# Regrouping the S5 branch of a hybrid layer by DMA through DRAM, with its convolutions, score chunks and decay selector rearranged

## Chip, cores and metric
The kernel runs on one core of one Trainium2 chip, as one program. The metric is the time of one execution on the device, in microseconds (us); the median of three executions is quoted.

## What is computed
A decoder layer for one sequence of 512 tokens with 1024 features: a gated feed-forward network, then a "hybrid mixer", then a second gated feed-forward network, each followed by a residual and a layer norm, and each modulated by a conditioning vector. The change lies in the mixer alone:

```python
proj = h @ w_in
z, xbc, dt_raw, u = split(proj)                    # 512 | 1024 | 8 | 512 columns
xbc = silu(causal_dwconv(xbc, conv_w, conv_b))     # 4 taps, per channel
xs, bm, cm = split(xbc)                            # 512 | 256 | 256
# SSD: chunks of 128 tokens, 8 heads; state passed from chunk to chunk
y_diag = (C B^T * exp(segsum(a*dt)))  @ (xs*dt)
y_off  = exp(cumsum(a*dt)) * C @ state_before
y_ssd  = rmsnorm((y_diag + y_off + d_ssd*xs) * silu(z)) * ssd_norm_w
# S5: 32 groups of 16 channels, 64 complex states each
x_t = A x_(t-1) + B u_t ;  y_t = Re(C x_t) + d*u_t
g = gelu(y_s5) ;  y_s5 = g * sigmoid(g @ w_glu + b_glu)
m = concat([y_ssd, y_s5]) @ w_out
```

All arrays are float32. Products of weights are made from a high and a low part (`split`, `mm3`): three matmuls in float32r for each product.

## The kernel before
The mixer (`mixer`, line 1248) holds features on the partitions and the 512 tokens along the row. A projection `proj()` makes one block of 128 columns of `w_in` for all tokens: 8 contraction tiles of 3 matmuls, into one PSUM bank. There are four such blocks for S5 (`u`), and eight for the convolutions (`conv(0)` to `conv(7)`; blocks 0 to 3 are `xs`, 4 and 5 `bm`, 6 and 7 `cm`).

S5 is worked four tokens at a time: 128 blocks of four tokens, so that one matmul contracts 4 tokens x 32 channels = 128 rows. For this the projected block, 128 channels x 512 tokens, must be regrouped to 4 tokens x 32 channels on the partitions, for each of four channel groups r. `s5_u` (line 930) does it with sixteen copies of 32 x 128 out of PSUM, twelve on ScalarE (L938) and four on VectorE (L940). `s5_scan` (line 942) makes eight matmuls (L949), a complex product with a rotation (`cmul`, three VectorE operations for each of the two parts), two scan instructions (L960) and a second `cmul`; its result X (two tiles, `bufs=1`) goes into `s5_y` (line 969): 48 matmuls (L978) that each load 32 columns of weights and write 32 PSUM partitions, so that the output lands in channel order, and one copy (L980). A float32 matmul is recorded as two passes. `s5_glu` (line 982) applies Gelu, splits, multiplies by `w_glu` (four contraction blocks into four banks) and applies Sigmoid.

For SSD, `ssd_dt` (line 1014) makes step sizes and decays; it is a generator that is advanced three times. `ssd_scores` (line 1117) makes for one chunk of 128 tokens C B^T, B transposed, and for each of two head groups a bank of decays: one matmul of the causal mask (L1132) and one with a selector of 64 rows (L1134: rows of `csel`, `acr`), then four Exp on ScalarE (L1137) and a product on VectorE. `ssd_x` transposes `xs`, `ssd_state` and `ssd_y` make state and output, `ssd_norm` and `ssd_out` the norm and the transposed result, which `out_proj` (line 1374) multiplies by `w_out`.

The text of `mixer` gives the order of priority: u, dt, u, scan, u, dt, scan, u, conv 4, dt, y0, conv 6, scan, conv 5, conv 7, y1, conv 0, scan, y2, conv 1, conv 2, y3 with Gelu, conv 3, then one chunk of scores, the gate product, and the other chunks. A planner fixes the order of each engine when the kernel is built: it takes, from what it holds to be ready by its own costs, what stands first in the text. `issue_after(i)` is an order on one engine only: what is traced in the block and runs on the engine of `i` is queued behind `i`. Each engine then works through its queue in order.

## Time and profile before

| | us |
|---|---|
| median of three executions | 966.65 (966.41 to 968.15) |
| profiled execution, its own time | 968.27 |
| its span, from the first to the last instruction | 966.6 |
| TensorE busy (98% of the span) | 944.9 |
| VectorE busy | 758.4 |
| ScalarE busy | 446.9 |
| GpSimd busy | 34.2 |

The mixer's part that the change touches runs from about 424 to 575 us of the span. Busy time of TensorE counts pipelined matmuls; how fast they follow each other is read from their start times in the timeline. In a timeline row the first number is the start, the second the duration from the first start to the last end of the instructions merged in the row, and brackets hold the idle time of the engine before it and what ended it. SPq and ACTq are the queues from which SyncE and ScalarE issue DMAs.

### The profile page before, as it was taken

The page shows a single profiled execution, that of the slowest core. Times are in us where ns is not written, and L with a number is a line of the kernel's source. Part 1 is how long each engine was busy: PE and PEld are TensorE (multiplying, and loading weights), DVE is VectorE, ACT ScalarE, POOL GpSimd, SP SyncE. Part 2 cuts the span into 40 slices and gives each one's busy share as a digit, 9 for nine tenths or more (in the row PEclk, how much of TensorE's full clock was granted, in tenths as well). Part 3 has the DMA queues.
Part 4 walks back from the last instruction along what each step waited for, and adds up shares of the span by engine and source line. Part 5 has one row for each costly group of instructions (what it writes and reads, how often), then busy time and mean ns, then how long its engine had stood idle before and what let it go on. Part 6 is the DMA issues. An engine that isn't in the chain of part 4 may idle for free.

```text
span 966.6 us, 14710 instructions
## 1 busy us (share of the span) xinstructions
PE 944.9 (98%) x5409; PEld 798.1 (83%) x5409; DVE 758.4 (78%) x1522; ACT 446.9 (46%) x879; POOL 34.2 (4%) x73
## 2 busy tenths in 40 slices
PE   8999999999999999999999999999999999999996
PEld 5778888887877888778877777988999999988885
DVE  6579998963677888858995889785788888896947
ACT  3343452635443335545537844533455554633420
POOL 0000000000000000100000110100000000000003
PEclk9999999999999999999999999999999999999999
DMA  9968584453866766362432024532233232543302
GB/s 342 377 190 270 188 280 162 157 174 122 261 204 197 242 217 180 86 233 71 142 121 67 1 88 152 173 111 66 88 99 120 89 129 90 175 152 109 109 1 87
DMA packets 75578, 147.93 MB, mean 153 GB/s; under 512 B 11633, under 2 KB 28657, under 8 KB 74993
## 3 DMA queue, kind: packets, MB, share of 16 engines
q1 hardware_dynamic: 75216, 146.94, 46.1%
q8 instruction: 42, 0.69, 0.3%
q14 instruction: 32, 0.25, 0.1%
q10 hardware_dynamic: 288, 0.04, 0.0%
HBM read 137.52 MB, written 9.44 MB: 152 GB/s over the span
## 4 chain that ended last, share of the span: by engine, by line
PE 86%; DVE 6%; ACT 4%; issue 2%; POOL 1%; DMA 0%; DVEq 0%; POOLq 0%; ACTq 0%
PE ps L103 27%; PE ps L104 27%; PE ps L105 27%; DVE cv L90 1%; PE ps L253 1%; PE ps L978 1%; DVE wlo L81 1%; PE ps L207 1%; ACT whi L96 1%; POOL rsx L170 1%; DVE s5X L81 0%; DMA raw<-in_w_in_dram 0%; PE ps L295 0%; DVE s5t L81 0%; PE ps L949 0%
## 5 line engine op out<-in xcount | busy, mean ns | idle before, releaser
L96 ACT CAST whi<-raw 128x1024 fp32r<-128x1024 f32 (+1 forms) x155 | 155.0, 1007 | 211.5 <-PE ps L104 97.5
L81 DVE TENSOR_TENSOR wlo<-raw,whi 128x1024 fp32r<-128x1024 f32 (+1 forms) x155 | 179.3, 1167 | 43.0 <-ACT whi L96 42.5
L103 PE MATMUL ps<-hT,whi 128*128 128x512 f32 x448 | 177.0, 396 | 1.7 <-ACT hT L1492 1.7
L104 PE MATMUL ps<-hT,whi 128*128 128x512 f32 x448 | 174.7, 390 | 0.1
L105 PE MATMUL ps<-hT,wlo 128*128 128x512 f32 x448 | 174.6, 390 | 0.0
L103 PE MATMUL ps<-whi,ghl 128*128 128x512 f32 x320 | 125.2, 391 | 0.0
L104 PE MATMUL ps<-wlo,ghl 128*128 128x512 f32 x320 | 124.5, 389 | 0.0
L105 PE MATMUL ps<-whi,ghl 128*128 128x512 f32 x320 | 124.3, 389 | 0.0
L103 PEld LDWEIGHTS ps<-hT,whi 128*128 128x128 f32 x448 | 83.9, 188 | 23.3 <-issue 3.2
L105 PEld LDWEIGHTS ps<-hT,wlo 128*128 128x128 f32 x448 | 84.1, 188 | 17.8
L104 PEld LDWEIGHTS ps<-hT,whi 128*128 128x128 f32 x448 | 84.2, 188 | 17.0 <-DVE hT L81 0.5
L103 PE MATMUL ps<-hx,whi 128*128 128x256 f32 (+1 forms) x320 | 97.5, 305 | 0.7 <-DVE cp L90 0.6
L104 PE MATMUL ps<-hx,whi 128*128 128x256 f32 (+1 forms) x320 | 97.3, 304 | 0.0
L105 PE MATMUL ps<-hx,wlo 128*128 128x256 f32 (+1 forms) x320 | 97.3, 304 | 0.0
L90 DVE SCALAR_TENSOR_TENSOR acc<-ra,cs,acc 128x1024 f32<-128x1024 f32 (+2 forms) x62 | 71.0, 1145 | 22.4 <-DMA ra<-in_w_ada_dram 21.9
L96 ACT CAST ghl<-g 128x512 fp32r<-128x512 f32 x88 | 53.1, 619 | 50.1 <-PE ps L105 37.5
L103 PEld LDWEIGHTS ps<-whi,ghl 128*128 128x128 f32 x320 | 60.1, 188 | 14.6 <-issue 2.5
L105 PEld LDWEIGHTS ps<-whi,ghl 128*128 128x128 f32 x320 | 60.1, 188 | 12.6
L104 PEld LDWEIGHTS ps<-wlo,ghl 128*128 128x128 f32 x320 | 60.1, 188 | 12.3
L81 DVE TENSOR_TENSOR ghl<-g,ghl 128x512 fp32r<-128x512 f32 x88 | 58.1, 686 | 13.6 <-ACT ghl L96 13.6
L103 PEld LDWEIGHTS ps<-hx,whi 128*128 128x128 f32 x320 | 61.1, 191 | 3.9 <-issue 0.8
L104 PEld LDWEIGHTS ps<-hx,whi 128*128 128x128 f32 x320 | 61.2, 191 | 2.6
(474 smaller groups left out, 1693.0 us busy)
## 6 DMA issues: line engine op xcount, KB each, us to landing
ra<-in_w_ada_dram SPq DMA_DIRECT2D x56, 512.0 KB, 4.5
raw<-in_up_dram SPq DMA_DIRECT2D x49, 512.0 KB, 4.2
raw<-in_ffn_w_dram SPq DMA_DIRECT2D x44, 512.0 KB, 4.4
raw<-in_up_dram SPq DMA_DIRECT2D x64, 256.0 KB, 3.8
ra<-in_ada_dram SPq DMA_DIRECT2D x16, 512.0 KB, 7.8
raw<-in_w_in_dram SPq DMA_DIRECT2D x16, 512.0 KB, 4.4
s5d<-s5mp SPq DMA_DIRECT2D x20, 256.0 KB, 3.8
s5M<-s5d SPq DMA_DIRECT2D x4, 1024.0 KB, 5.1
```

Source lines behind the costliest of these rows:

```text
L81: self.nc.vector.tensor_tensor(out=out, in0=a, in1=b, op=op)
L90: self.nc.vector.scalar_tensor_tensor(out=out, in0=a, scalar=s, in1=b, op0=op0, op1=op1, **k)
L96: keep(self.nc.scalar.copy(out=hi, in_=src))
L103: mm(o, lh, rh, start=first, stop=False, **k)
L104: mm(o, lh, rl, start=False, stop=False, **k)
L105: self.last_mm = mm(o, ll, rh, start=False, stop=last, **k)
L170: self.nc.gpsimd.tensor_scalar(out=x, in0=var, scalar1=EPS, scalar2=None, op0=ADD)
L207: self.nc.tensor.matmul(ps, self.onesr, bc(self.onesr, (1, 4)), start=True, stop=True)
L253: nc.tensor.matmul(bank[q:q + 32, 0:256], lhs, w[:, :, m * P:(m + 1) * P], start=(j < 2), stop=(j >= len(put) - 2))
L978: nc.tensor.matmul(pv[32 * r:32 * r + 32, j, :], M[:, n, r, 32 * j:32 * j + 32], rhs[:, r, :], start=(n == 0), stop=(n == 2))
```

## The change
- **Regrouping.** `s5_u` becomes one ScalarE copy of the bank (with tokens regrouped along the row) into a tile `s5c`, followed by `s5_turn`: one DMA of 256 KB from the ScalarE queue into a DRAM tile, and four DMAs of 64 KB from the GpSimd queue that read it back with 32 partitions each. `s5_y` becomes 12 matmuls with all 128 columns of weights, one copy, and the same turn; its result lands in the buffer of U, in regrouped order, and Gelu writes it into G in channel order.
- **Scan.** The constant tiles `d0` and X are made once; vr and vi take one buffer of the shared tag `t4` (two buffers) in place of tiles of their own.
- **Order.** Conv 4 and 6 stand between the second u and the first scan; the order is then scan, u, scan, u, conv 5, y0, scan, conv 7, conv 0, y1, scan, conv 1, y2, conv 2, conv 3, y3. Two chunks of scores stand ahead of the gate product, a third is queued behind the last Gelu; three Gelu are queued behind the Exp of the second chunk, and the Sigmoids behind the Exp of the last chunk. The weight loads are reordered to match.
- **Selector.** `acr` gets 128 rows for each head group, the other group's 64 rows filled with zeros (two more ScalarE operations), and L1134 uses all 128 rows.

```diff
+    def s5_turn(self, b, n, src, out):
+        d = self.s5_turns[b][:, n]
+        self.nc.scalar.dma_start(out=d, in_=src)
+        for j in range(4):
+            self.nc.gpsimd.dma_start(out=out[32 * j:32 * j + 32],
+                                     in_=d[:, j].rearrange("(r c) t -> c r t", r=4))
-    def s5_u(self, U, ups):
-        uv = ups.rearrange("p (t i) -> p i t", i=4)
-        for r in range(4):
-            for ii in range(4):
-                o, a = U[32 * ii:32 * ii + 32, r, :], uv[32 * r:32 * r + 32, ii, :]
-                if (r + ii) % 4 < 3:
-                    nc.scalar.copy(out=o, in_=a)
-                else:
-                    nc.vector.tensor_copy(o, a)
+    def s5_u(self, b, sp, U, ups):
+        c = sp.tile([P, 4, P], F32, tag="s5c", bufs=1, name=self.nm("s5c"))
+        self.nc.scalar.copy(out=c, in_=ups.rearrange("p (t i) -> p i t", i=4))
+        self.s5_turn(b, 0, c, U)
...
-        for j in range(4):
+        for r in range(4):
             for n, rhs in enumerate((U, X[0], X[1])):
-                for r in range(4):
-                    nc.tensor.matmul(pv[32 * r:32 * r + 32, j, :], M[:, n, r, 32 * j:32 * j + 32],
-                                     rhs[:, r, :], start=(n == 0), stop=(n == 2))
-        return nc.scalar.copy(out=G, in_=ps).ins
+                nc.tensor.matmul(ps[:, r, :], M[:, n, r, :], rhs[:, r, :], start=(n == 0), stop=(n == 2))
+        c = sp.tile([P, 4, P], F32, tag="s5c", bufs=1, name=self.nm("s5c"))
+        i = nc.scalar.copy(out=c, in_=ps).ins
+        self.s5_turn(b, 1, c, G)
...
+        def gelu(k):
+            return nc.scalar.activation(G[k].rearrange("p (t j) -> p j t", j=4), T[k], AF.Gelu_apprx_tanh).ins
         with self.tc.issue_after(after):
-            for k in range(4):
-                nc.scalar.activation(G[k], G[k], AF.Gelu_apprx_tanh)
+            gelu(0), gelu(1)
+            last = gelu(2)
         split(0), split(1)
+        with self.tc.issue_after(last):
+            self.last_gelu = gelu(3)
...
-            nc.scalar.activation(s, pss[o], AF.Sigmoid, bias=self.col["b_glu"][:, o:o + 1])
+            with self.tc.issue_after(self.last_exp):
+                nc.scalar.activation(s, pss[o], AF.Sigmoid, bias=self.col["b_glu"][:, o:o + 1])
...
-            gl = slice(64 * g, 64 * g + 64)
-            nc.tensor.matmul(ps, self.csel[gl, c, :], self.acr[gl], start=False, stop=True)
+            nc.tensor.matmul(ps, self.csel[:, c, :], self.acr[:, g], start=False, stop=True)
...
                 u()
+                next(dt)
+                conv(4)
+                conv(6)
                 scan()
                 u()
-                next(dt)
+                next(dt, None)
                 scan()
-                u(), conv(4)
-                next(dt, None)
+                u(), conv(5)
                 y(0)
-                conv(6)
                 scan()
-                conv(5), conv(7)
+                conv(7)
+                conv(0)
                 y(1)
-                conv(0)
                 scan()
+                conv(1)
                 y(2)
-                conv(1)
                 conv(2)
+                i = conv(3)
+                y(3)
                 mixT = []
-                glu = self.s5_glu(G, mixT, y(3))
-                next(glu)
-                i = conv(3)
...
                 with tc.issue_after(i):
                     scores()
+                scores()
+                glu = self.s5_glu(U, G, mixT, self.last_exp)
+                next(glu)
+                with tc.issue_after(self.last_gelu):
+                    scores()
+                tr()
                 next(glu), next(glu)
+                scores()
                 next(glu), next(glu)
-                tr()
-                scores(), scores()
```

## Rows read from the trace of the kernel before
**Rows 1.** The page's line of busy times by engine: busy us, share of the span, instructions.
```profile
PE 944.9 (98%) x5409; PEld 798.1 (83%) x5409; DVE 758.4 (78%) x1522; ACT 446.9 (46%) x879; POOL 34.2 (4%) x73
```
**Rows 2.** Busy time in chosen stretches: the stretch, its length, then busy us (and instructions) of PE, PEld, DVE, ACT, POOL, the granted TensorE clock as a share of full speed, the DMA share, GB/s.
```profile
424.20:513.10 88.90, 85.78 (x738) 70.49 (x736) 75.87 (x126) 43.68 (x93) 2.76 (x11) 0.98 0.41 142
513.10:546.60 33.50, 33.15 (x171) 25.21 (x168) 20.30 (x31) 30.37 (x65) 2.04 (x4) 1.00 0.10 32
...
480.00:492.80 12.80, 12.58 (x153) 10.42 (x153) 12.80 (x18) 6.49 (x9) 0.17 (x3) 1.00 0.24 72
495.30:499.20 3.90, 3.87 (x80) 3.72 (x80) 3.90 (x6) 1.30 (x2) 0.00 (x0) 0.58 0.55 188
```
**Rows 3.** What TensorE waited for between 425 and 600 us: us in total, times, longest.
```profile
PE ps L978 <- DVE s5X L81: 2.3, 2, 2.1
PE ps L1219 <- DVE zs L85: 1.9, 3, 0.7
```
**Rows 4.** TensorE's timeline at y1 (481.95), y2 (492.16) and y3 (510.35), with the projections that follow the first two and the scan before y2.
```profile
481.95 0.43 PE L978 MATMUL ps<-zx,s5M 128*32 128x128 f32 x8
...
484.71 0.50 PE L103 MATMUL ps<-hT,whi 128*128 128x512 f32 x1
...
490.28 1.95 PE L949 MATMUL ps<-zx,s5M 128*128 128x128 f32 x16
492.16 0.43 PE L978 MATMUL ps<-zx,s5M 128*32 128x128 f32 x8
...
495.33 0.65 PE L978 MATMUL ps<-s5X,s5M 128*32 128x128 f32 x8 [2.08 <-DVE s5X L81]
...
499.23 0.50 PE L103 MATMUL ps<-hT,whi 128*128 128x512 f32 x1
...
510.35 0.42 PE L978 MATMUL ps<-zx,s5M 128*32 128x128 f32 x8
```
**Rows 5.** TensorE's timeline at the first scan's matmuls, with the projection that follows.
```profile
440.26 1.95 PE L949 MATMUL ps<-zx,s5M 128*128 128x128 f32 x16
441.96 0.48 PE L103 MATMUL ps<-hT,whi 128*128 128x512 f32 x1
```
**Rows 6.** TensorE's timeline at the end of conv 3's projection and through the first chunk of scores.
```profile
518.45 0.39 PE L105 MATMUL ps<-hT,wlo 128*128 128x512 f32 x1
518.68 0.38 PE L1123 MATMUL ps<-zx 128*128 128x128 f32 x2
...
519.34 0.38 PE L1132 MATMUL ps<-mask,identb 128*128 128x512 bf16 x1
519.64 0.50 PE L1134 MATMUL ps<-acr,csel 64*128 64x512 f32 x1
520.08 0.39 PE L1132 MATMUL ps<-mask,identb 128*128 128x512 bf16 x1
```
**Rows 7.** TensorE's timeline from the state of one chunk (L1168) to the first product of the output projection.
```profile
542.87 1.03 PE L1168 MATMUL ps<-sx,bt 128*128 128x256 f32 x4
...
546.63 0.58 PE L103 MATMUL ps<-whi,mixT 128*128 128x512 f32 x1
```
**Rows 8.** ScalarE's timeline: three Gelu, conv 3's first pass, the first copy behind its Silu, the load of the Exp table and the Exp of the first chunk.
```profile
519.02 1.67 ACT L993 ACTIVATE zx<-zx 128x512 f32<-128x512 f32 x3
...
521.62 0.77 ACT L1111 ACTIVATE cv<-ps,cols 128x512 f32<-128x512 f32 x1
...
527.67 0.35 ACT L1127 COPY cbt<-ps 128x256 f32<-128x256 f32 x1
...
528.31 1.28 ACT L1137 ACT_TABLE_LOAD   x1
529.61 2.17 ACT L1137 ACTIVATE E<-ps,nacs 128x128 f32<-128x128 f32 x8
```
**Rows 9.** Groups of instructions by line between 424 and 513 us: line, engine, operation, tiles, shapes, count, then busy us, mean ns of one, idle time before them and what ended it; VectorE's first, then ScalarE's.
```profile
L940 DVE COPY zx<-ps 32x128 f32<-32x128 f32 x16 | 4.6, 287 | 1.6 <-ACT zx L938 1.2
L90 DVE SCALAR_TENSOR_TENSOR cv<-ps,cols,cv 128x510 f32<-128x510 f32 x6 | 4.5, 746 | 0.0
...
L938 ACT COPY zx<-ps 32x128 f32<-32x128 f32 x48 | 12.3, 256 | 11.4 <-DVE zx L940 10.9
```
**Rows 10.** Of the instructions that read the tile s5M, those of the scans' first product: min, median and max ns, first and last start.
```profile
L81 DVE TENSOR_TENSOR s5vr<-s5M,ps x4: 674/682/689, 442.9 to 496.9; 128x512 f32<-128x512 f32 x4
```
**Rows 11.** DMA issues of the whole execution: count, size, median us from issue to landing.
```profile
s5d<-s5mp SPq DMA_DIRECT2D x20, 256.0 KB, 3.8
...
s5d<-Er SPq DMA_DIRECT2D x4, 256.0 KB, 2.5
...
ew<-in_up_dram SPq DMA_DIRECT2D x2, 64.0 KB, 4.3
s_b_re<-in_s_b_re_dram SPq DMA_DIRECT2D x2, 64.0 KB, 2.9
```
**Rows 12.** GpSimd's timeline, the same operation on 128x2 elements twice, and what VectorE ran beside the first.
```profile
552.72 0.86 POOL L170 TENSOR_SCALAR rsx<-ss 128x2 f32<-128x2 f32 x1 [5.92 <-ACT jk L1207]
...
573.32 0.22 POOL L170 TENSOR_SCALAR rsx<-ss 128x2 f32<-128x2 f32 x1 [4.69 <-ACT jk L1207]
...
552.81 0.68 DVE L81 TENSOR_TENSOR y<-y,sx 128x512 f32<-128x512 f32 x1
574.36 0.62 DVE L85 TENSOR_SCALAR zs<-zs,ssr 128x256 f32<-128x256 f32 x2 [2.13 <-POOL ssr L171]
```

More of the change, by code (lines that the diff above doesn't have):

```diff
@@ L951, in s5_scan @@
         mk = lambda n: sp.tile([P, 4, P], F32, tag="s5" + n, bufs=1, name=self.nm("s5" + n))
-        d0, vr, vi = mk("d0"), mk("vr"), mk("vi")
+        if b == 0:
+            self.s5_d0, *self.s5_x = mk("d0"), mk("X0"), mk("X1")
+            for a in (self.s5_d0, *self.s5_x):
+                nc.gpsimd.memset(a[:, :, 0:1], 0.0)
+        d0, X = self.s5_d0, self.s5_x
+        v2 = self.tmp.tile([P, 1024], F32, tag="t4", name=self.nm("s5v")).rearrange("p (n r t) -> p n r t", n=2, r=4)
+        vr, vi = v2[:, 0], v2[:, 1]
         t = self.tmp.tile([P, 512], F32, tag="t2", name=self.nm("s5t")).rearrange("p (r t) -> p r t", r=4)
-        nc.scalar.copy(out=d0, in_=bc(self.s5_m4[:, 4 * b:4 * b + 4], (2, P)))
-        nc.gpsimd.memset(d0[:, :, 0:1], 0.0)
+        nc.scalar.copy(out=d0[:, :, 1:], in_=bc(self.s5_m4[:, 4 * b:4 * b + 4], (2, P - 1)))
         Er, Ei = M[:, 2], M[:, 3]
@@ L960, in s5_scan @@
             nc.vector.tensor_tensor_scan(out=fl(v), data0=fl(d0), data1=fl(v), initial=0.0, op0=MUL, op1=ADD)
-        X = [sp.tile([P, 4, P], F32, tag=f"s5X{n}", bufs=1, name=self.nm("s5X")) for n in range(2)]
-        for x in X:
-            nc.gpsimd.memset(x[:, :, 0:1], 0.0)
         s = slice(0, P - 1)
@@ L1082, in ssd_dt @@
         self.tt(bd, bc(pt, (1, NH)), bc(self.hsel, (2, P)), MUL)
-        self.acr = dp.tile([P, 4, P], F32R, name="acr")
+        self.acr = dp.tile([P, 2, 4, P], F32R, name="acr")
         for g in range(2):
-            self.split(bd[:, 4 * g:4 * g + 4], self.acr[64 * g:64 * g + 32], self.acr[64 * g + 32:64 * g + 64])
+            a = self.acr[:, g]
+            self.split(bd[:, 4 * g:4 * g + 4], a[64 * g:64 * g + 32], a[64 * g + 32:64 * g + 64])
+            o = slice(64 - 64 * g, 128 - 64 * g)
+            nc.scalar.mul(out=a[o], in_=bc(self.ones[o], (1, 4)), mul=0.0)
         self.dt, self.nacs, self.eacs, self.etot, self.dec = dt, nacs, eacs, etot, dec
@@ L1237, in want_mixer @@
                       self.zw_alloc)
-        cols = [1544 + b * P for b in range(4)] + [512 + b * P for b in (4, 6, 5, 7, 0, 1, 2, 3)]
+        cols = [1544, 1544 + P] + [512 + b * P for b in (4, 6)] + [1544 + b * P for b in (2, 3)]
+        cols += [512 + b * P for b in (5, 7, 0, 1, 2, 3)]
         for c0 in cols:
@@ L1294, in u @@
                     U.append(Ub[len(U)])
-                    self.s5_u(U[-1], proj())
+                    self.s5_u(len(U) - 1, sp, U[-1], proj())
                 def scan():
@@ L1302, in y @@
                 def y(b):
[L1303 removed]
+                    i = self.s5_y(b, sp, M[1][b], U[b], X[b], U[b])
                     load(1)
@@ L1355, in mixer @@
                 tr()
-                scores()
                 for _ in glu:
@@ L1527, in body @@
         L.s5_m4 = L.cp.tile([P, 16], F32, name="s5m4")
+        L.s5_turns = [tc.dram_tile([P, 2, 4, P], F32, name=f"s5t{b}") for b in range(4)]
         L.s5_dram = [tc.dram_tile([P, 7, 4, P], F32, name=f"s5d{b}") for b in range(4)]
```

13 lines of the change are left out of this document (6 added, 7 removed).

## Prediction
> **What bounds the kernel now.** The page comes first: TensorE is busy for 98% of the span [rows 1], so a change pays where it takes work from TensorE or closes one of the few places where TensorE waits; what leaves another engine pays only if TensorE waits for it. Next, the busy times by stretch over the mixer [rows 2]: from 424.2 to 513.1 TensorE is busy 85.78 of 88.90 us and VectorE 75.87, and from 480 VectorE has no idle time at all, so in this stretch both are close to the bound; from 513.1 to 546.6 TensorE is busy 33.15 of 33.50 us although ScalarE has 30.37 us of work there: the planner finds TensorE other work. Then the waits of TensorE [rows 3]: the largest is y2 waiting 2.3 us for the scan's result X on VectorE, then 1.9 us in three waits of the last transposes. Last, TensorE's timeline, where the starts of consecutive matmuls show what one really costs.
>
> **y2's wait.** y1 takes 484.71 - 481.95 = 2.76 us; y2 takes 499.23 - 492.16 = 7.07 [rows 4]. Of the 4.31 us between them 2.3 are the wait; the rest is the half-speed stretch behind it, with a granted clock of 0.58 of full speed from 495.3 to 499.2 [rows 2], between the levels of 1.2 and 2.4 GHz, after TensorE had stood for 2 us. In the new order two projections or more stand between a scan and its y, and VectorE loses the sixteen copies of L940, 4.6 us [rows 9]. Credit: **4.3**, if X is then in time.
>
> **Is it?** Before, VectorE's scan work began at 442.9 [rows 10], 2.6 us after the first scan's matmuls at 440.26 [rows 5], and y3 started at 510.35 [rows 4]. A projection takes 490.28 - 484.71 = 5.57 us [rows 4]. Conv 4 and 6 ahead of the first scan put it 2 x 5.57 = 11.1 us later; what VectorE need no longer do after that is 4.6 of copies and most of six convolution passes of 0.75, 4.5 [rows 9]. So the last X comes at 510.35 + 11.1 - 9.1 = 512.4. TensorE would be ready for y3 at 511.0 (next parts: conv 3 used to end at 518.68 [rows 6]; less 4.3 and 0.8 that gives 513.5 for y3's end, and 2.55 for y3). X is 1.4 us late, bounded by 0 and 5, since the count leaves out any idle time of VectorE. What is ready meanwhile is scores, which need only conv 4 to 7. I count nothing, and keep up to 3.6 as a rival.
>
> **y on full columns.** Before, 48 matmuls of 32 columns in 2.76 us [rows 4]. After, 12 matmuls, 24 passes; sixteen such passes take 441.96 - 440.26 = 1.70 us [rows 5], so 2.55. Four times 0.21: **0.8**. The lower end is 0, the column groups having run side by side already.
>
> **Selector.** From the mask matmul to the next pair is 520.08 - 519.34 = 0.74 us, of which 0.44 lie behind the 64-row matmul; a 512-column matmul on all rows passes in 518.68 - 518.45 = 0.23 [rows 6]. A pair on all rows should take 0.46. Eight pairs by 0.28: **2.2**. The lower end is 0 (the gap could come from the bfloat16 mask ahead). The Trainium skill, page "TensorEngine Tiling (Array Packing)", section "When to Use Tiling", speaks against this edit: at a contraction of 64 or less it advises two row tiles, up to twice as fast. Its "Key Properties" say that a change of tiling mode drains the engine, and the trace agrees with that: the two tiles never run side by side, a full-row mask matmul stands between them. By the first rule alone eight halves of 0.23 would be lost, 0.9, instead of 2.2 gained.
>
> **ScalarE and the small edits.** ScalarE loses 12.3 us of copies and 11.4 us of standing for VectorE between them [rows 9], and gets four copies of a whole bank and two of zeros. Gelu, Silu, Exp and Sigmoid no longer alternate: loads of 1.28 us [rows 8] fall away. TensorE waited for none of this but 0.35 us in 513.1 to 546.6 [rows 2], so the credit is 0; it shifts Exp and Sigmoid earlier. The tiles d0 and X made once free GpSimd of small memsets; vr and vi in `t4` share two buffers with the Gelu splits, which come after the scans. Weight loads on SyncE's queue follow the new order and stay ahead by the same count. All 0; uncovered, the zeros would cost about 1.2.
>
> **The turns.** None of this is in the trace: GpSimd issues no DMA before. A 256 KB write lands in 2.5 to 3.8 us, a 64 KB load in 2.9 to 4.3 [rows 11]. With a copy of 0.6, a turn takes from 6.0 (loads side by side) to 0.6 + 3.8 + 4 x 4.3 = 21.6 (one after another). I take 10, nearer to the first, as 64 KB loads need not wait for each other. Queued behind the wait: on ScalarE only what follows the write's issue, which waits for the copy just before it; on GpSimd, in order, the four loads behind the write's landing, with the later memsets of xd and the two selections for `csel` behind them; all of those are wanted tens of us later. SyncE's queue is passed by nothing. The cover for U is the order: between the third u's end and its scan TensorE has a scan, two projections and a y: 1.70 + 2 x 5.57 + 2.55 = 15.4 us; the other u have 18 or more. So 0, up to a turn of 15.4. Without that cover each turn would stand open, 10 us.
>
> **The new wait.** Conv 3 and y3 have changed places, and the gate product now waits for Exp. Call y3's end Z (513.5). Conv 3's projection ends at Z - 2.55. From there to its Silu's end took 527.67 - 518.68 = 9.0 us before [rows 6, 8], with a crowded ScalarE; free, it is a pass of 0.77, three of 0.75 and a Silu of about 0.6: 3.6. Behind it on ScalarE, in order: the Exp table 1.28, two chunks of 2.83 (copies from 527.67, Exp to 531.78, less the load), the Gelu table 1.28, three Gelu 1.67, a cast of 0.6 [rows 8]: 10.5. The first gate matmul comes at Z + 11.5 (to 17.0). TensorE's cover by the text's order is three score chunks, 0.66 + 2 x 0.46 = 1.6 each [rows 6], and four transposes: 5.2. That leaves a wait of 6.3 to 11.8. If the planner draws the fourth chunk and the state and output of two chunks forward, 3.76 each (542.87 to 546.63 [rows 7]), the cover is 13.8 and the wait 0 to 3.2. The full TensorE of 513.1 to 546.6 [rows 2] speaks for the second. I take **2.0**. Gelu 3, which waits for y3's turn, comes behind the other Gelu at Z + 11 and is needed only by the fourth quarter of the product.
>
> **Sum.** 4.3 + 0.8 + 2.2 - 2.0 = 5.3. The profiled execution took 968.27 with a span of 966.6, 1.6 above the median; I take the difference from the median: 966.65 - 5.3 = **961.4**.
>
> **Rivals.** (a) The gate wait takes the place of y2's: the planner keeps the text's order, or conv 3's Silu is late. Wait 6.3 to 11.8: 966 to 971, likeliest 967. Against: TensorE's filled stretch. (b) Slower: turns above 15.4 us, because GpSimd issues late beside VectorE. The same GpSimd operation took 0.22 us while VectorE stood and 0.86 while it added two tiles [rows 12]; VectorE is nearly full here. At 21.6 the third scan comes 6.2 late, Gelu 3 holds ScalarE and costs TensorE about 3, and the clock falls again, 2: 966.65 - 5.3 + 11.2 = 972.6. It decides from 15.4 on. The Trainium skill, "GPSIMD Engine Reference", section "Specifications", states this contention for VectorE instructions with two SBUF inputs, and "DMA: Bandwidth & Descriptors", "SWDGE vs HWDGE vs iDMA", that GpSimd writes descriptors into SBUF; that descriptors are slowed is shown by no row here. (c) VectorE becomes the bound: X late by 5 at y3, 3.6 of it uncovered: 965.0. (d) All waits close: no gate wait, and the 1.9 us of the last transposes [rows 3] go too, as Exp and Sigmoid end earlier: 966.65 - 7.3 - 1.9 = 957.4.
>
> **How the numbers follow.** Forecast (959 to 964) 0.50; (a) 0.16; (b) 0.12; (c) 0.10; (d) 0.12. The measurement tells about 0.2%, 1.9 us, from no change. Faster: 0.50, (d), half of (c) and a quarter of (a): 0.71. Same: half of (c), 0.07 of (a): 0.12. Slower: (b) and 0.05 of (a): 0.17. The range reaches from (d) into (a), 957 to 968; left out are (b) and the ends of (a) and (d), 0.19.
>
> **What would show it.** Right: TensorE's wait for X under 1 us and the clock at full speed through the scans; y in about 2.6 us; mask to next pair in about 0.46; turns of about 10 us; a gate wait near 2. Wrong: starts of scans that wait for a DMA, a gate wait above 6, or X later than y3's turn.

## The result, and the profile after

| | time, us | ratio to before, 95% interval |
|---|---|---|
| before, five runs | 966.95 (966.41 to 968.20) | |
| after, five runs | 978.64 (975.78 to 979.68) | 1.0111 (1.0090 to 1.0132) |
| forecast | 961.4 (957 to 968) | |

The change makes the kernel 11.7 us slower; the forecast had the sign wrong and the time lies outside its range. The profiled execution of after is the one of 975.78.

The page of after, its span and its busy line:

```profile
span 974.0 us, 14137 instructions
PE 939.9 (96%) x5121; PEld 797.0 (82%) x5121; DVE 752.7 (77%) x1506; ACT 434.8 (45%) x833; POOL 50.0 (5%) x96
```

Beside [rows 1] every large engine has less to do (TensorE too), and yet the span is longer: the time is in waits. Those of TensorE from 424 to 640 us (from the mixer to the transposes behind it), with total, count and longest:

```profile
PE ps L103 <- ACT ghl L96: 7.6, 1, 7.6
PE ps L979 <- DVE s5X L81: 3.3, 2, 3.1
PE ps L339 <- DVE res L87: 3.2, 2, 2.7
PE ps L104 <- DVE hx L81: 1.7, 1, 1.7
...
PE ps L1162 <- ACT E L1148: 0.9, 1, 0.9
...
PE ps L951 <- DMA zx<-s5t: 0.6, 1, 0.6
```

The waits of [rows 3] have not closed but moved: the gate product waits 7.6 us for a cast on ScalarE, a y waits 3.1 for X where y2 waited 2.3, and a third group (L339, L104) stands behind the mixer, of which the prediction says nothing. The turns, the new risk, cost one wait of 0.6. The busy times by stretch (columns as in [rows 2]):

```profile
440.00:450.00 10.00, 10.00 (x48) 8.34 (x47) 3.86 (x6) 3.51 (x6) 2.17 (x4) 1.00 0.55 157
470.00:516.00 46.00, 42.08 (x244) 36.23 (x245) 46.00 (x63) 15.75 (x22) 6.50 (x12) 1.00 0.54 168
521.00:530.30 9.30, 0.82 (x6) 0.43 (x5) 3.97 (x7) 9.27 (x24) 3.27 (x6) 0.69 0.18 47
530.30:534.70 4.40, 4.40 (x10) 3.19 (x11) 1.95 (x3) 4.37 (x10) 0.00 (x0) 0.50 0.00 0
```

VectorE has 3.86 us of work in the first ten and then no idle time at all for 46 us. TensorE stands in the third stretch while ScalarE is full, and in the fourth its granted clock is 0.50, the level of 1.2 GHz: the nine gate matmuls from 530.29 to 534.59 start 0.48 us apart in the mean, where 0.23 is usual [rows 6], which makes 2.2 us more. ScalarE's timeline shows what it does in that time:

```profile
518.34 0.63 ACT L1127 ACTIVATE zx<-cv 128x512 f32<-128x512 f32 x1 [1.06 <-DVE cv L90]
...
519.52 1.28 ACT L1148 ACT_TABLE_LOAD   x1
520.81 3.46 ACT L1148 ACTIVATE E<-ps,nacs 128x128 f32<-128x128 f32 x13
...
525.61 1.28 ACT L996 ACT_TABLE_LOAD   x1
526.90 2.90 ACT L996 ACTIVATE zx<-zx 128x512 f32<-128x512 f32 x3
529.61 1.14 ACT L96 CAST ghl<-zx 128x512 fp32r<-128x512 f32 x2
```

Conv 3's Silu (518.34) waits for VectorE; behind it in order come two chunks of Exp, the Gelu, and only then the cast that the gate needs. VectorE's timeline, the end of the second scan's X and conv 3's three passes, and TensorE's (a y that reads X, two pieces of the last y, two mask matmuls of one pair, the first gate matmul):

```profile
477.59 0.68 DVE L81 TENSOR_TENSOR s5X<-s5X,s5t 128x508 f32<-128x508 f32 x1
...
516.00 2.30 DVE L90 SCALAR_TENSOR_TENSOR cv<-ps,cols,cv 128x511 f32<-128x511 f32 x3
```

```profile
478.41 0.46 PE L979 MATMUL ps<-s5X,s5M 128*128 128x128 f32 x2 [3.08 <-DVE s5X L81]
...
514.93 0.39 PE L979 MATMUL ps<-zx,s5M 128*128 128x128 f32 x2
...
515.60 0.39 PE L979 MATMUL ps<-zx,s5M 128*128 128x128 f32 x2
...
516.94 0.38 PE L1144 MATMUL ps<-mask,identb 128*128 128x512 bf16 x1
...
517.39 0.39 PE L1144 MATMUL ps<-mask,identb 128*128 128x512 bf16 x1
...
530.29 0.79 PE L103 MATMUL ps<-ghl,whi 128*128 128x512 f32 x1 [7.62 <-ACT ghl L96]
```

The first of these y is that of scan 0, and it waits for scan 1's X. X is now one pair of tiles made in the first scan, and the text puts scan b+1 ahead of y b: so a y reads what the next scan has written (y3 excepted). This is a change of what is computed, not only of the order; it holds for the kernels made from after unless "own X" is said. The time does not hang on it: e2, which gives each scan its own X again, takes 978.33.

**Where the time went.** Each kernel enters the mixer at its own time (the first matmul of dt starts at 429.65 in before and 427.62 in after), so I count from that matmul (e8 shows where the difference comes from). Stages: to the first mask matmul (all projections, scans, y); from there to the output projection's first matmul (gate, chunks); from there to the end of the span. The first column is the start of the first scan's matmuls. The medians of before beside the experiments were 966.5 to 967.9.

| kernel | first scan at | scans | gate | rest | sum | median |
|---|---|---|---|---|---|---|
| before | 10.60 | 89.68 | 27.30 | 419.92 | 536.90 | 966.95 |
| after | 21.85 | 89.31 | 35.62 | 421.47 | 546.40 | 978.64 |
| e1 selector alone | 10.60 | 89.69 | 26.03 | 419.90 | 535.62 | 967.31 |
| e2 own X | 21.86 | 86.62 | 39.23 | 421.10 | 546.95 | 978.33 |
| e3 Gelu first | 21.86 | 89.35 | 34.48 | 422.00 | 545.83 | 977.25 |
| e4 no turns | 23.30 | 92.99 | 34.27 | 422.67 | 549.93 | 979.05 |
| e5 gate order back | 21.86 | 90.16 | 41.23 | 420.58 | 551.97 | 982.20 |
| e6 the same, own X | 21.86 | 89.38 | 36.49 | 421.68 | 547.55 | 978.31 |
| e7 splits held | 21.86 | 90.11 | 34.85 | 417.83 | 542.79 | 973.44 |
| e8 before again | 10.60 | 89.70 | 27.30 | 419.91 | 536.91 | 967.10 |
| e9 product first | 21.86 | 90.06 | 33.84 | 421.45 | 545.35 | 975.91 |
| e10 Gelu early | 21.86 | 90.10 | 33.23 | 422.18 | 545.51 | 975.81 |
| e11 early, own X, held | 21.86 | 86.62 | 34.68 | 418.71 | 540.01 | 971.06 |
| e12 order alone | 23.31 | 93.14 | 29.81 | 419.90 | 542.84 | 972.82 |
| e13 scan sooner | 16.42 | 88.22 | 36.18 | 421.01 | 545.42 | 976.41 |
| e14 sooner, own X, held | 16.41 | 84.92 | 32.74 | 419.24 | 536.90 | 968.10 |
| e15 Gelu at conv 1 | 16.41 | 84.93 | 32.73 | 418.68 | 536.34 | 967.79 |
| e16 before, u on ScalarE | 13.42 | 88.16 | 26.06 | 420.46 | 534.68 | 964.75 |
| e17 the same, not the first u | 10.63 | 85.41 | 26.08 | 420.47 | 531.96 | 961.83 |
| e18 the same, last two u | 10.62 | 86.67 | 26.20 | 420.48 | 533.35 | 963.53 |

After minus before is -0.37 + 8.32 + 1.55 = 9.50 us by stage. The other 2.2 of the 11.7 between the medians are in no stage shown here: after's profiled execution is its shortest, and it entered the mixer early, as e8's did.

Two kernels of the table lie between before and after, so the difference can be taken in three steps (scans, gate, rest, sum; us):

| step | scans | gate | rest | sum |
|---|---|---|---|---|
| before to e12: the new order of the scan stage | +3.46 | +2.51 | -0.02 | +5.94 |
| e12 to e4: the gate's new order, y3 behind conv 3, X made once, the selector | -0.15 | +4.46 | +2.77 | +7.09 |
| e4 to after: the turns and y on full columns in place of the copies | -3.68 | +1.35 | -1.20 | -3.53 |

The first two steps lose 13 us, and the turns give 3.5 of them back. The price of a step holds in this sequence; in another it could differ.

### The profile page after: what moved, and what is told of

Same layout as the page of the kernel before. It is cut to its first block, busy times and chain, and to the rows that moved or that the text cites. A ratio compares the mean times of both kernels' runs of the same rounds, so it can differ in the third digit from the quotient of the medians.

```text
span 974.0 us, 14137 instructions
## 1 busy us (share of the span) xinstructions
PE 939.9 (96%) x5121; PEld 797.0 (82%) x5121; DVE 752.7 (77%) x1506; ACT 434.8 (45%) x833; POOL 50.0 (5%) x96
## 4 chain that ended last, share of the span: by engine, by line
PE 78%; DVE 12%; issue 3%; DMA 3%; ACT 2%; POOL 1%; SPq 0%; DVEq 0%; POOLq 0%; ACTq 0%
PE ps L103 25%; PE ps L104 25%; PE ps L105 25%; DVE wlo L81 1%; DVE cv L90 1%; DVE s5v L967 1%; DVE s5v L81 1%; DVE s5t L81 1%; DMA ew<-in_up_dram 1%; DVE s5X L81 1%; DVE st L672 1%; DVE res L90 1%; DMA raw<-in_up_dram 1%; DVE res L87 1%; DMA b_ada<-in_badaT_dram 0%
## 5 line engine op out<-in xcount | busy, mean ns | idle before, releaser
L104 PE MATMUL ps<-hT,whi 128*128 128x512 f32 x448 | 174.9, 390 | 0.1
L104 PE MATMUL ps<-wlo,ghl 128*128 128x512 f32 x320 | 124.5, 389 | 0.0
L104 PEld LDWEIGHTS ps<-hT,whi 128*128 128x128 f32 x448 | 84.2, 188 | 17.0 <-DVE hT L81 0.5
L104 PE MATMUL ps<-hx,whi 128*128 128x256 f32 (+1 forms) x320 | 97.4, 304 | 0.0
L105 PEld LDWEIGHTS ps<-whi,ghl 128*128 128x128 f32 x320 | 60.0, 188 | 12.7
L104 PEld LDWEIGHTS ps<-wlo,ghl 128*128 128x128 f32 x320 | 60.1, 188 | 12.3
L103 PEld LDWEIGHTS ps<-hx,whi 128*128 128x128 f32 x320 | 61.1, 191 | 3.9 <-issue 0.8
L105 PEld LDWEIGHTS ps<-hx,wlo 128*128 128x128 f32 x320 | 61.1, 191 | 2.5
```

The costliest lines, as they stand in the source:

```text
L103: mm(o, lh, rh, start=first, stop=False, **k)
L104: mm(o, lh, rl, start=False, stop=False, **k)
L105: self.last_mm = mm(o, ll, rh, start=False, stop=last, **k)
```

## The experiments

**The theory after the result**: (i) ScalarE's queue, Exp ahead of Gelu, opens the gate's wait; (ii) a y tied to the next scan's X, and VectorE standing after 440 because the first scan comes later, take the gain of the scan stage; (iii) waits behind the mixer come from weight halves (of the next layer's weights). Rivals: the turns, or VectorE's or ScalarE's amount of work as such.

### e1, the selector alone, and e8, before once more

```diff
-            nc.tensor.matmul(ps, self.csel[gl, c, :], self.acr[gl], start=False, stop=True)
+            nc.tensor.matmul(ps, self.csel[:, c, :], self.acr[:, g], start=False, stop=True)
```

> The kernel before with the 128-row selector alone (its zeros included; the scans' vr and vi share the buffers of t4, as in the changed kernel, since the larger selector leaves no room for tiles of their own). Theory: the 0.44 us behind each 64-row matmul become 0.22, eight pairs give 2.2 us: 964.7. Rival 1: the gap came from the bfloat16 mask ahead, nothing changes: 967. Rival 2: half-row tiles were the better use of the array, 0.9 us slower: 968. The mask matmul to the next pair should show 0.46 in place of 0.74.

Measured: 967.31, ratio 0.9999 (0.9989 to 1.0009). In after a pair takes 517.39 - 516.94 = 0.45 us, as forecast, and TensorE's busy time in e1's profile is 2.27 less than in before's. But the stages give back only 1.28: TensorE's waits in the gate stage grow (for the gate's cast from 0.4 to 0.8 us, and 0.4 at a chunk's output). The medians do not show the 1.28; the two profiled executions, which enter the mixer within 0.06 us of each other, do: 967.04 against 968.27.

e8 is the kernel before, unchanged.

> The kernel before, profiled once more. Its waits around y2 and at the last transposes should stand as they did, and the span at 965 to 967; if stages move by more than 1 us between two profiles of the same kernel, differences of that size in the other profiles mean nothing.

Its stages agree with the first profile's to 0.02 us, its entry into the mixer does not: 427.89 against 429.65. The 1.7 us arise ahead of the mixer's change, at the projection of z, where TensorE waits 1.14 us in both; behind that wait the granted clock fell in the first profile (0.66 of full speed over the next 5 us, between its two levels of 1.2 and 2.4 GHz) and not in this one (1.00). Before's line, then e8's:

```profile
399.50:404.50 5.00, 5.00 (x15) 3.95 (x16) 4.36 (x8) 3.10 (x7) 1.02 (x2) 0.66 0.36 109
399.00:404.00 5.00, 4.78 (x21) 3.97 (x22) 4.68 (x9) 3.43 (x8) 0.70 (x2) 1.00 0.34 108
```

In all twenty profiles the ten matmuls behind that wait take either 2.2 us, and the mixer is entered at 427.6 to 428.4, or 3.3 to 3.8, and it is entered at 429.3 to 429.8, whatever the kernel: times can differ by about 1.7 us for this alone. Most of the 2.2 us above may be that; the executions without a profile do not show it.

The scan stage can move in the same way. e7, e9 and e10 leave after's scan stage as it is, and take 90.06 to 90.11 against 89.31: behind the first y's wait of about 3 us the granted clock fell in these three (0.67 or 0.68 over the next 5 us), and not in after and e3 (1.00). After's line, then e7's:

```profile
478.40:483.60 5.20, 5.19 (x34) 4.74 (x35) 5.20 (x9) 1.58 (x2) 0.00 (x0) 1.00 0.78 267
478.50:483.80 5.30, 5.25 (x21) 4.42 (x22) 5.30 (x9) 0.78 (x1) 0.00 (x0) 0.68 0.77 269
```

So in kernels with that wait, differences of up to 0.8 us in the scan stage mean nothing; elsewhere stages can be compared between single profiles more closely.

### e2, each scan its own X

```diff
...
-        d0, X = self.s5_d0, self.s5_x
+        d0 = self.s5_d0
...
+        X = [sp.tile([P, 4, P], F32, tag=f"s5X{n}", bufs=1, name=self.nm("s5X")) for n in range(2)]
+        for x in X:
+            nc.gpsimd.memset(x[:, :, 0:1], 0.0)
```

> The changed kernel, but each scan allocates its own X (one buffer, column 0 zeroed each time), as before the change. Theory: the waits of the first y come from its reading tiles that the next scan in the text writes; with tiles of its own y follows its own scan, and the 3.1 us wait goes: 975.5 (974 to 976.5), the gate's wait of 7.6 us unchanged. Rival: VectorE is simply late; the next scan's X waits for y to free the one buffer, the same microseconds come back as waits of the later y: 978 to 980.

Measured: 978.33, in the rival's range. The first y no longer waits and the scan stage is 2.69 us shorter, as the theory had it, though y2 now waits 2.0 for X; the gate stage is 3.61 longer, which neither said. ScalarE's line for conv 3's Silu:

```profile
519.09 0.63 ACT L1129 ACTIVATE zx<-cv 128x512 f32<-128x512 f32 x1 [1.53 <-DVE cv L90]
```

It starts 519.09 - 428.37 = 90.72 us after dt's first matmul, in after 518.34 - 427.62 = 90.72: to the hundredth the same, although TensorE ended its projections sooner: the Silu waits for VectorE, which makes conv 3's passes. The first gate matmul follows 11.95 us behind that Silu in both (531.04 and 530.29). What TensorE gains before is waited for at the gate.

### e3, Gelu ahead of Exp, and e9, the product ahead of the chunks too

```diff
...
-                with tc.issue_after(i):
+                glu = self.s5_glu(U, G, mixT, i)
+                next(glu)
+                with tc.issue_after(self.gelu2):
                     scores()
                 scores()
-                glu = self.s5_glu(U, G, mixT, self.last_exp)
                 next(glu)
```

> The changed kernel, but the first three Gelu go ahead of the Exp of the two chunks on ScalarE; the fourth Gelu goes behind those Exp. Theory: the gate product waits 7.6 us because ScalarE does 16 Exp and a table load ahead of the Gelu; with the Gelu first, the first gate matmul comes 7 to 8 us after the end of y3 in place of 14, with 5 to 6 us of other work of TensorE in between: the wait is 2 to 3, the stretch at half clock behind it goes, 970 to 972. Rival: ScalarE as a whole is the bound of this stretch, the Exp are then late for the states and outputs, and the wait only moves: 977 to 979.

Measured: 977.25, in the rival's range; of the gate's 35.62 us only 1.14 go. TensorE's timeline of e3:

```profile
522.28 0.58 PE L1146 MATMUL ps<-acr,csel 128*128 128x512 f32 x1
527.84 0.59 PE L1145 MATMUL ps<-mask,identb 128*128 128x512 bf16 x1 [4.98 <-ACT bt L1141]
...
530.30 1.12 PE L1163 MATMUL ps<-ident,zx 128*128 128x128 f32 x4 [1.44 <-ACT E L1149]
531.33 0.79 PE L103 MATMUL ps<-ghl,whi 128*128 128x512 f32 x1
```

The casts are there 5.6 us sooner (526.11 - 429.76 = 96.35 after dt, in after 529.61 - 427.62 = 101.99), but three chunks and the transposes lie ahead of the product in TensorE's own queue, and their banks come free only by ScalarE's copies, now behind the Gelu. e9 puts them behind the product as well:

```diff
...
-                with tc.issue_after(i):
-                    scores()
-                scores()
-                glu = self.s5_glu(U, G, mixT, self.last_exp)
-                next(glu)
+                self.conv3 = None
+                glu = self.s5_glu(U, G, mixT, i)
+                next(glu), next(glu)
                 with tc.issue_after(self.last_gelu):
                     scores()
+                next(glu), next(glu)
+                next(glu), next(glu)
                 tr()
-                next(glu), next(glu)
-                scores()
-                next(glu), next(glu)
+                scores(), scores()
...
```

> The changed kernel, its scan stage untouched; behind conv 3's Silu come all four Gelu, then the Exp, and TensorE has the gate product behind one chunk of scores, the other two chunks behind the product. Theory: e3 freed the Gelu alone and TensorE's queue held the product back; e5 held conv 3's Silu back instead. With both in order the first gate matmul comes about 8 us after the end of y3 (Silu 2.7, load 1.3, two Gelu 2.2, cast 0.6) with 1.6 to 2 of cover, a wait of 5 to 6 at once, but the Exp and the later chunks are then covered by the product: the state comes 3 us earlier, 974 to 976. Rival 1: Gelu 3 waits for the turn of y3 (11 us) and holds every Exp back in ScalarE's queue; the time is found again before the state: 978 to 981. Rival 2: the wait for the gate is lost whole (as I forecast at first): 970 to 972.

Measured: 975.91, inside the theory's range. The gate's waits are 5.0 in place of 7.6 and the first state matmul comes 3.8 sooner (113.74 after dt against 117.56), but the stage shortens by 1.78 only.

### e4, the new order without the turns

```diff
...
-        c = sp.tile([P, 4, P], F32, tag="s5c", bufs=1, name=self.nm("s5c"))
-        self.nc.scalar.copy(out=c, in_=ups.rearrange("p (t i) -> p i t", i=4))
-        self.s5_turn(b, 0, c, U)
...
+        for r in range(4):
+            for ii in range(4):
...
```

> The changed kernel in its order, but u and y regroup as before the change (sixteen copies of 32 partitions into U, y on column groups, Gelu in place), with no DMA through DRAM. Theory: the turns are hidden but for a wait of 0.6 us, and the copies cost VectorE 4.6 us again, so this is not faster: 978 to 981, waits for X longer than 3.1. Rival: the turns are the loss, by late U, by the transfers or by the Gelu with regrouped output: 968 to 973.

Measured: 979.05, in the theory's range, though the wait for X is 2.4 and not longer than 3.1. The scan stage is 3.68 us longer than in after and all three stages together 3.53: the turns cost less than the copies and column groups that they replace. They are not the loss.

### e5 and e6, the gate's order of before

```diff
...
-                i = conv(3)
-                y(3)
                 mixT = []
+                glu = self.s5_glu(U, G, mixT, y(3))
+                next(glu)
+                self.conv3 = conv(3)
+                next(glu)
...
```

> The changed kernel, but the gate goes back to its place of before: y3 ahead of conv 3, Gelu 0 and 1 ahead of conv 3's Silu, Gelu 2 and 3 right behind that Silu and ahead of the first Exp, one chunk of scores ahead of the gate product on TensorE and the other three after or within it. Theory: e3 gained little since TensorE's own queue still had three chunks of scores and four transposes ahead of the gate product, and their banks come free only by ScalarE; with the product first, it covers the Exp: no wait above 2 us at the gate, no half clock, 968 to 971 (the later waits of 3 stay). Rival: the stretch is bound by ScalarE's sum, or the turns of y2 and y3 (11 us) come too late for Gelu 2 and 3: the wait is found again inside the gate product, 975 to 978.

Measured: 982.20, slower than both. ScalarE's timeline of e5:

```profile
519.17 0.59 ACT L981 COPY s5c<-ps 128x512 f32<-128x512 f32 x1 [4.57 <-DMA s5t<-s5c]
...
531.59 1.28 ACT L1128 ACT_TABLE_LOAD   x1 [2.51 <-DVE cv L90]
...
534.83 2.04 ACT L996 ACTIVATE zx<-zx 128x512 f32<-128x512 f32 x2
```

y3's copy waits 4.57 us for the landing of y2's write, as both use the one buffer s5c; two Gelu, a Silu and three table loads behind it hold conv 3's first pass back to 527.37 and its Silu to 532.88, and Gelu 2 and 3, behind that Silu, hold the second half of the product. My theory was wrong here: the old order does not carry the turns. The gate's first wait is 6.5 us, and the product's second half comes late as well, as the rival said, but dearer than it said.

e6 is e5 with the edit of e2.

> As e5, and each scan has its own X (one buffer) as in e2. Theory: in e2 the scan stage ended 2.7 us earlier, and the gate gave it back because ScalarE's chain there, counted from conv 3, set the time; with the gate covered the 2.7 us stay: 2 to 3 us under e5, 965.5 to 968. Rival: the earlier end of the scans only lengthens the wait for the turns of y2 and y3 or for VectorE: same as e5 within 1 us.

Measured: 978.31: outside both ranges. Own X is worth 4.4 here in the sum, where y3's copy no longer waits for the landing of y2's write.

### e7, three weight halves behind the drain

```diff
...
-            ws = [(self.wnext(), self.wnext()) for _ in range(halves)]
+            with self.tc.issue_after(self.dr1[0]):
+                ws = [(self.wnext(), self.wnext()) for _ in range(halves)]
...
```

A drain is VectorE's work that takes a finished bank of the output projection into the residual; `dr1[0]` belongs to the first drain of the second half.

> The changed kernel, but three halves of the next layer's weights are kept behind the first drain of the second half of the output projection on VectorE (an order alone; nothing is left out). Theory: the waits of 2.7, 0.5 and 1.7 us at the transposes of res and at hx come from these halves, whose loads land late, in front of that drain: they shrink to about 1, and the kernel is 3 us faster: 975 to 976.5. Rival: the drains are late anyway, since the output projection itself ends late, or the weights are then late: 978 to 980.

In after VectorE's timeline ahead of the first drain of the second half reads:

```profile
592.72 1.22 DVE L81 TENSOR_TENSOR wg<-raw,wg 128x1024 fp32r<-128x1024 f32 x1 [0.72 <-ACT wg L96]
596.07 1.23 DVE L81 TENSOR_TENSOR wlo<-raw,whi 128x1024 fp32r<-128x1024 f32 x1 [2.12 <-ACT whi L96]
597.22 0.68 DVE L81 TENSOR_TENSOR dr<-ps,gate 128x512 f32<-128x512 f32 x1
```

Measured: 973.44, faster than the theory's range. The rest is 3.64 us shorter than in after, and the waits are

```profile
PE ps L339 <- DVE res L87: 0.5, 1, 0.5
PE ps L104 <- DVE hx L81: 0.4, 1, 0.4
```

in place of 3.2 and 1.7. The planner had drawn halves whose loads land late ahead of the drain (ScalarE waits 4.64 and 2.30 us for these loads). The change does not touch these lines; that their place moved because what stands ahead of them did is inferred, not tested.

### e10 and e11, Gelu early, and all three causes at once

```diff
...
-                conv(2)
-                i = conv(3)
+                mixT = []
+                glu = self.s5_glu(U, G, mixT, conv(2))
+                next(glu)
+                self.conv3 = conv(3)
                 y(3)
-                mixT = []
...
```

> As e9, but Gelu 0 and 1 go behind conv 2's Silu, ahead of conv 3's, since their turns have long landed; Gelu 2 and 3 behind conv 3's Silu, one chunk of scores ahead of the product. Theory: half of the product is ready when TensorE has ended y3, and covers the Silu, the other Gelu and the turn of y3: no wait above 1.5 us at its start, 1 to 3 within it: 969 to 972. Rival: two more table loads delay conv 3's Silu, and Gelu 3's wait for the turn of y3 holds the Exp: 975 to 978.

Measured: 975.81, the rival's range. The gate's wait is down to 1.6, but the later mask matmuls wait for Exp, and the gate stage is 33.23.

e11 is e10 with the edits of e2 and e7.

> e10 with the two other causes taken away as well: each scan its own X (e2) and the three halves of weights behind the first drain (e7). Theory, with the causes adding up: under e10 by 2.7 (own X, stays now that the gate is covered) and by 3.6 to 5 (splits): 962 to 966, level with the kernel before or faster. Rival: the gains overlap (an earlier end of the scans only waits longer for the turns): 967 to 970.

Measured: 971.06, ratio 1.0032 (1.0021 to 1.0043): above both ranges. Beside e10, own X takes 3.48 from the scans (0.8 of it is e10's fallen clock) and adds 1.45 to the gate; the held splits take 3.47 from the rest. Both causes are real, but taking them away does not make the kernel faster than before.

### e12, the order alone

```diff
...
                 u()
+                next(dt)
+                conv(4)
+                conv(6)
                 scan()
                 u()
-                next(dt)
+                next(dt, None)
                 scan()
...
```

> The kernel before with the new order of the scan stage alone: conv 4 and 6 ahead of the first scan, the other convolutions between a scan and its y; u and y regroup by copies and column groups, y3 ahead of conv 3, the gate and the selector as before. Theory: the projections between scan and y close the wait of y2 (2.3 us and 2 of half clock), but VectorE does the same work in the same stretch, and its first scan starts 11 us later: X comes late at the end instead, and the end of the scan stage moves by less than 1 us: 966 to 968. Rival: the order alone brings the 4.3 us that I credited to it: 962.5.

Measured: 972.82, ratio 1.0046 (1.0029 to 1.0063): outside both, slower. Lines of its waits and its busy times:

```profile
PE ps L978 <- DVE s5X L81: 4.1, 3, 2.2
...
PE ps L1060 <- DVE adt L90: 1.1, 1, 1.1
```

```profile
440.00:450.00 10.00, 8.94 (x42) 7.15 (x41) 5.06 (x15) 6.58 (x19) 0.00 (x0) 1.00 0.19 52
```

Before's line of the same stretch:

```profile
440.00:450.00 10.00, 10.00 (x64) 8.94 (x63) 9.55 (x21) 6.31 (x20) 0.00 (x0) 1.00 0.20 52
```

The order that was to close y2's wait makes three of it. VectorE has 5.06 us of work where before had 9.55, and is full from 490 to 516. The gate stage, whose order is that of before, is 2.51 us longer.

### e13 to e15, the first scan sooner

```diff
                 conv(4)
-                conv(6)
                 scan()
                 u()
                 next(dt, None)
+                conv(6)
                 scan()
```

> The changed kernel, but conv 6 goes behind the second u's scan instead of ahead of the first (its weights too), so that the first scan comes one projection, 5.6 us, sooner; U of the first scan still has 11 us for its turn. Theory: VectorE stood 6.1 us of the 10 from 440 to 450 and was full from 470 to 516; the sooner scan fills that hole, X and the convolutions of the end come 3 to 5 us sooner, conv 3's Silu and the gate with them: 973.5 to 976. Rival: what limits is the turns or the wait for the next scan's X, the hole is closed and nothing moves: 978 to 980.

```profile
440.00:450.00 10.00, 10.00 (x54) 8.56 (x53) 5.38 (x9) 2.38 (x7) 2.17 (x4) 1.00 0.54 157
```

```profile
517.42 0.63 ACT L1127 ACTIVATE zx<-cv 128x512 f32<-128x512 f32 x1 [1.07 <-DVE cv L90]
```

Measured: 976.41, the direction of the theory but less. VectorE does 1.52 us more in those ten, conv 3's Silu starts 517.42 - 428.00 = 89.42 after dt, 1.30 sooner, and the first gate matmul 1.29 sooner: what closes of the hole, a quarter of its 6.1 us, comes back almost whole.

e14 is e11 with this edit; e15 is e14 with Gelu 0 and 1 made behind conv(1) in place of conv(2).

> e11 with conv 6 behind the first scan. Theory as for e13: VectorE's late start was what e11 still paid: 3 to 5 us under e11's 971.1: 966 to 968. Rival: e11's rest (3 us over the kernel before) is the gate's 5.3 us wait for Gelu behind conv 2's Silu, and a sooner scan changes it by less than 1: 970 to 971.

Measured: 968.10, ratio 1.0001 (0.9992 to 1.0010): 3.0 under e11, a tenth above the theory's range. Its scans take 84.92, 4.76 less than before; the gate stage takes 5.44 more, with these waits among others:

```profile
PE ps L103 <- ACT ghl L96: 2.7, 1, 2.7
...
PE ps L1142 <- DVE y L81: 1.5, 1, 1.5
```

> e14, and Gelu 0 and 1 go behind conv 1's Silu in place of conv 2's, their casts later as the buffers come free. Theory: the gate's wait at its start goes, 2 to 4 us under e14: 963 to 966. Rival: the Gelu holds up the convolutions' Silu by two table loads of 1.28, no better than e14.

Measured: 967.79. The gate matmul starts 2.88 sooner and the gate stage is the same to 0.01: the rival. Wherever its first wait stood, the gate stage stayed at some 33 us in e10, e14 and e15; what holds it there was not tested.

### e16 to e18, VectorE relieved in the order of before

```diff
-                if (r + ii) % 4 < 3:
+                if late or (r + ii) % 4 < 3:
                     nc.scalar.copy(out=o, in_=a)
```

These are e17's and e18's lines: `late` is true for all but the first u in e17, for the last two in e18. In e16 the branch is gone, and ScalarE makes every copy. All three have e1's selector, so they are compared with e1.

> The kernel before with the 128-row selector (e1) and all sixteen copies of a u on ScalarE, four fewer on VectorE. No DMA, no new order. Theory: VectorE is relieved of 4.6 us in the stretch where it is full from 480 on, X of the third scan comes sooner, and y2's wait of 2.3 with the half clock behind it closes; U comes 1.2 us later where nothing waits for it: 2 to 4 us under e1: 962 to 965. Rival: the copies are longer on ScalarE alone, the scans themselves wait for U: 967 to 971.

Measured: 964.75, ratio 0.9966 (0.9954 to 0.9978), in the theory's range. y2's wait is gone; a wait at dt is new, behind the first u's copies on ScalarE:

```profile
430.61 4.27 ACT L937 COPY zx<-ps 32x128 f32<-32x128 f32 x16
434.90 0.57 ACT L1025 COPY dtfm<-ps 16x512 f32<-16x512 f32 x1
```

```profile
PE ps L1028 <- ACT dtfm L1025: 2.0, 1, 2.0
```

> e16, but the first u is copied by both engines as before the change, the other three by ScalarE alone. Theory: the 2.0 us wait of dt's matmul and the 2.8 us at the first scan were the first u's copies ahead of dt's copy in ScalarE's queue; they go, y2's wait stays closed: 2 to 3 us under e16, 961.5 to 963. Rival: the 2.8 us of delay at the first scan lie beside VectorE's work, and y2 waits again in their place: 964 to 965.

Measured: 961.83, ratio 0.9956 (0.9944 to 0.9969), the fastest kernel of the study. The scan stage takes 85.41, 4.28 less than e1's. The stretch around y2, before's line and then e17's:

```profile
490.00:500.00 10.00, 7.68 (x117) 6.70 (x117) 10.00 (x15) 3.46 (x6) 0.21 (x2) 0.83 0.77 280
490.00:500.00 10.00, 10.00 (x132) 8.56 (x132) 9.97 (x14) 2.73 (x5) 0.21 (x2) 1.00 0.20 66
```

> e16, but only the last two u are copied by ScalarE alone. Theory: as e17, but VectorE is relieved of half as much; y2's wait comes back in part: 962 to 965, not faster than e17. Rival: only the last two u lie where VectorE is full, and it equals e17.

Measured: 963.53: in the theory's range, between e1 and e17, as is its scan stage (86.67, with a wait for X of 0.8). Each u whose copies leave VectorE counts.

## Why the prediction was wrong, by its own steps

Two steps failed. In the scan stage (forecast -5.1 us, measured -0.37) "Is it?" counted VectorE as if it always had work, and making X once was priced at nothing. At the gate (forecast -0.2 with the selector, measured +8.32) I chose the wrong one of two covers.

**y2's wait, +4.3: size right, means wrong.** The wait with its half clock is worth what I took: e17 closes it and gains 4.28. The new order does not close it: e12 has waits of 4.1 for X. In "Is it?" I set 11.1 us of delay against 9.1 us that VectorE need no longer do, as if VectorE had work all the time. From 440 to 450 it had 3.86 us in after, and e13, which fills 1.52 of that hole, is 1.30 sooner at conv 3's Silu. I had written that the count leaves out idle time, and still bounded it at 5. The 9.1 were too much as well: the first u's four copies (1.1 us) lay ahead of the first scan's VectorE work in before, and conv 6's three passes (2.2) still ran behind its start in after.

The last X itself came in time for y3; what came late were the convolution passes behind it on VectorE, and with them conv 3's Silu. I looked only at X.

**X made once, 0: wrong.** I took it for a saving of memsets. With one pair of tiles each y but the last waits for the next scan's X, 3.1 us at the first and 3.3 in all; e2 takes that wait away and its scan stage is 2.69 shorter. Of the 4.7 us by which after's scan stage exceeds the forecast (89.31 against 84.6) these 3.3 are the largest part; 0.6 are a wait for a turn and 0.5 the smaller gain of y.

**y on full columns, +0.8: too much.** A quarter takes 515.60 - 514.93 = 0.67, four take 2.68, against 2.76 before: 0.1 each, 0.3 in all.

**Selector, +2.2: right for TensorE's work, too much for the time.** 0.45 us a pair, 2.27 us less work, 1.28 less in the stages (e1). The Trainium skill's advice in "TensorEngine Tiling (Array Packing)", "When to Use Tiling", two row tiles at a contraction of 64, does not hold for this place: a pair takes 0.45 us on all rows against 0.74 [rows 6], and e1 is not slower.

**Turns, 0: right but for 0.6.** In after's trace the eight turns take 6.7 to 12.7 us from the start of the copy to the landing of the last read, 10.4 in the mean; I took 10. The third u's copy starts at 457.64 and its scan at 470.57, 12.9 us later, with a wait of 0.6: the cover was not 15.4, as y0, which I had counted in it, stood waiting for X and came behind the scan. Rival (b) falls with e4.

**The gate's wait, -2.0: the step that decided.** The working gave 6.3 to 11.8 by the text's order and 0 to 3.2 if the planner pulls work forward; I chose the second. (Its cover adds up to 14.3 and not 13.8, which makes 0 to 2.7; nothing hangs on it.) TensorE's queue has just the three chunks and four transposes, then stands 7.6, and loses 2.2 more at the half clock. "The full TensorE of 513.1 to 546.6" was no evidence: there the gate product itself stood ahead of three of the four chunks and covered their Exp, and the change puts three chunks ahead of the product. The first gate matmul came 14.0 us after y3's end, not 11.5: conv 3's Silu ended 2.7 after it, not 1.1, as its first pass waited 0.9 behind a weight cast on ScalarE and the others 0.7 for VectorE, and three Gelu that write regrouped took 2.90, not 1.67. Rival (a) came true in its wait; of rival (c), VectorE was the bound, but it made conv 3's passes late, not X at y3.

That the order of Exp and Gelu alone makes the gate's loss, theory (i), is not shown. Gelu first gives back 1.14 us of the stage (e3), the product ahead of two chunks 1.78 in all (e9), Gelu early 2.39 (e10). 2.51 come with the order of the scans and before's own gate (e12), and 4.46 with the gate's new order and its companions (e12 to e4), although the selector saves some 1.3 among them. No gate behind the turns took less than 32.7, against 27.3 before.

**Behind the mixer, 0: not looked at.** 1.55 us net; with the splits held 3.64 come back (e7).

By stage: I forecast -5.1 for the scans and -0.2 for gate and chunks; measured were -0.37 and +8.32, and +1.55 behind. With own X and a sooner scan the scans take 84.92 (e14), against 89.68 - 5.1 = 84.6 forecast.

What stays open: how much of the 2.2 us by which the medians differ more than the stages is the clock ahead of the mixer; and what keeps the gate stage of e14 and e15 at 33 us.

## What to carry to other kernels

Before moving the first piece of a chain later, ask what its engine does until then: if the engine is full afterwards, that idle time came back as delay in this kernel, and a sum of busy times does not show it. A stretch in which TensorE never waits does not say that another order will be filled as well: see which work covers which, and if the change moves the covering work to the other side, price the wait by the text's order. A tile made once in place of once per pass ties each reader to the last writer ahead of it in the text: look at what is read, and at what is waited for. And try the small edit first: twelve small copies moved from the full engine to one with room (e17) brought 4.3 of the 5.1 us that a new order and full columns were to bring in the scan stage.

## What the runs showed of the hardware

Sixteen copies of 32 partitions, shared between ScalarE and VectorE in before, run from 430.58 to 436.13, 5.5 us, with ScalarE standing for VectorE's copies in between; ScalarE alone takes 4.27 (e16). A Gelu that writes regrouped (every fourth element apart) takes 1.14 us alone and 2.90 for three in a row, against 0.63 and 1.67 for plain ones. A turn through DRAM (after) is a copy of 0.6, a write that lands after 4.7 (median), four issues on GpSimd of 0.55 each, and reads that land after 2.4 (median): 6.7 to 12.7 us from copy to the last landing. Waits of one length did not always bring the lower clock: behind 1.14 us at the projection of z it fell in the first profile of before and not in e8, the same kernel.
